# The down projection of a decoder trunk by seven half-size products, with weights moving and tokens as rows

## The chip, the cores and the metric

One core of one Trainium2 chip runs the whole trunk. The metric is device time in microseconds from launch to end; lower is better. Three runs of the kernel before were timed, and one further execution was profiled.

## The reference

For 512 tokens of width 2048 the trunk computes a token mixer, a residual, a SwiGLU feed-forward block, a second residual and a last RMSNorm, all in float32. The change concerns the second half:

```python
    h = h + mix @ w_out                       # (512, 2048), w_out (2048, 2048)
    xn = rms_norm(h, ffn_norm_w)
    ff = silu(xn @ w_gate) * (xn @ w_up)      # (512, 5632)
    h = h + ff @ w_down                       # w_down (5632, 2048)
    return rms_norm(h, final_norm_w)
```

## The kernel before

**Precision.** A float32 operand is split into a rounded part and a rest, both in the format fp32r (`split`: ScalarE writes the first, VectorE subtracts for the second), and each product takes three TensorE instructions (`mm3`, lines 147 to 149): high by high, high by low, low by high. In the names of the trace `wh`, `wl` are the parts of a weight tile, `hh`, `hl` those of the normed input, `sh`, `sl` those of its sums, `fh`, `fl` those of the feed-forward activations. "mm<-fh,wh" names the moving operand first and the standing one second.

**Layout.** Activations lie with features on the 128 partitions and 512 tokens along the row. Weight tiles stand in the array and tokens move, in most stages. In the early stage of `rows_tiles` it is the other way: tokens stand, weights move.

**Stages.** `project` computes h + mix @ w_out in 16 tiles of 128 features; it stores h to DRAM (`hd`, from ScalarE's queue), keeps a copy times the norm's weights (`hf`) and the split parts (`hw`), and sums squares on GpSimd. `project_end` adds the squares over partitions on TensorE and makes the norm's factors. The norm's division is applied later: gate and up are multiplied by `rstd`, h is multiplied by `rms`, and the last norm divides both out.

Gate/up then runs over 44 tiles f, each with one gate and one up tile of 128 columns. The first two are plain (`ff_plain`). The other 42 (`ff_fast`) halve tokens, contraction and the pair gate/up, and replace eight half-size products by seven, with sums of the operands: the token sums are made once (`token_sums`), the weight sums per tile on VectorE (lines 784, 786, 787, 794). Four raw weight tiles of 128x1024 give seven split weight tiles. The order of the products is 11, 12, S2, S1, S3, 22, S4; two of the four PSUM banks accumulate more than one product, so that a bank must be read between two of them. `put_ff` (lines 732 to 735) applies the norm and silu, and stores u to DRAM (`ffd`, 256 KB, from SP's queue).

Down (`down_all`) loads h back (16 loads of 256 KB on ScalarE's queue), multiplies it by `rms` (line 895), loads the activations in chunks of eight tiles and splits them (`ff_load`), and for each chunk runs the 16 output tiles, eight k-tiles each, with an add into h (line 816). The last chunk of four tiles (`down_last`) runs over two token halves of 256, so that the last norm of the first half lies beside the products of the second. The last norm is squares on ScalarE, a sum on VectorE, one TensorE instruction over partitions, a small chain, and a multiplication per tile; the stores go out on SP's and ScalarE's queues.

**Order and buffers.** Instructions are traced in program order; a scheduler then fixes each engine's order by priority and by its own estimate of time. `high_priority(offset=6000)` lets weight loads, sums and splits run ahead of what the program has before them; a negative offset holds work back. Each engine works its queue in that fixed order. Ahead of the products run three split weight tiles (`wh`, `wl`, three buffers each) and five raw ones. A new tile in a buffer's place waits until the readers of the old one are done.

Of the kernel before, what the change touches and what calls it, by code (L numbers as in the profile page):

```python
# [27 lines left out]
GF = 4  # L28
CF = 8
NCHUNK = NF // CF  # L30
PLAIN = 2
HALF = 256
NB = S // P
# [11 lines left out]
POOL_OUT = (0, 4)  # L45
# [8 lines left out]
def _layout_cols():  # L54
    at = 0
    for name, n in (
        ("attn_w", 16), ("q_w", 4), ("kv_w", 4), ("mla_w", 1), ("conv_w", 4 * CONV_W),
        ("conv_b", 4), ("ln_w", 4), ("ln_b", 4), ("lower", HG), ("hgrn_w", 1),
        ("ffn_w", 16), ("final_w", 16), ("inv_freq", 1), ("sign", 1), ("eps", 1),
        ("ln_eps", 1), ("half_pi", 1),  # L60
    ):
        _COLS[name] = (at, n)
        at += n
    return at
# [30 lines left out]
class Trunk:  # L95
# [574 lines left out]
    def project(self, w, r4):  # L670
# [3 lines left out]
        self.hd = self.dp.tile([KT, P, S], F32, name="hd")  # L674
        sq_sum = self.sq_sum = r4("acc")
        for m in range(KT):
            t = self.hf[:, m]
            nc.sync.dma_start(t, self.io["x"][m])
            bank = self.cols_tile(w, self.mix_y + self.mix)
            nc.vector.tensor_tensor(t, t, bank, op=ALU.add)  # L680
            nc.scalar.dma_start(self.hd[m], t)
            self.hw.append(self.split(t, self.hp("hh", F32R), self.hp("hl", F32R), self.col("ffn_w", m)))
            if m == 0:
                nc.scalar.activation(sq_sum, t, AF.Square)
            else:
                q = r4("sq")
                nc.scalar.activation(q, t, AF.Square)
                nc.gpsimd.tensor_tensor(sq_sum, sq_sum, q, op=ALU.add)
            nc.scalar.activation(t, t, AF.Copy, scale=self.col("ffn_w", m))

    def project_end(self, r4):
# [3 lines left out]
        y, q, v = r4("sq"), self.rstd, r4("acc")  # L695
        nc.vector.tensor_scalar(self.rms, total, 1.0 / D, self.col("eps"), op0=ALU.mult, op1=ALU.add)
        r = self.rsqrt(total, D, "eps", v, y, q)
        nc.vector.tensor_scalar(self.epsv, self.rms, EPS, None, op0=ALU.mult)
        nc.vector.tensor_tensor(self.rms, self.rms, r, op=ALU.mult)
        nc.vector.tensor_copy(self.rstd, r)  # L700
# [3 lines left out]
    def token_sums(self, sp, tp):  # L704
# [4 lines left out]
        H = {i: (sp("sh", F32R, (P, n, HALF)), sp("sl", F32R, (P, n, HALF))) for i in (1, 2, 3, 4)}  # L709
# [19 lines left out]

    def put_ff(self, f, g, u):  # L730
# [4 lines left out]
        nc.sync.dma_start(self.ffd[f], u)  # L735

    def ff_plain(self, f, w, fp):
        nc = self.nc
        gbank = self.cols_tile(w, self.hw)
        ubank = self.cols_tile(w, self.hw)  # L740
        g, u = fp("g"), fp("u")
# [3 lines left out]
        nc.sync.dma_start(self.ffd[f], u)  # L745

    def ff_fast(self, f, w, rp, fp):
# [4 lines left out]
        with self.tc.high_priority(offset=6000):  # L752
            b11, b21, b12, b22 = raws = [rp("raw", F32, W) for _ in range(4)]
# [21 lines left out]
        g, u = fp("g"), fp("u")  # L775
# [7 lines left out]
        def sums():  # L783
            tt(b11, b12, b11, op=ALU.subtract)
            t2 = rp("t2", F32, W)
# [16 lines left out]
        self.put_ff(f, g, u)  # L802


    def ff_load(self, k, fp):
        nc = self.nc
        with self.tc.high_priority(offset=3000):
            t = fp("fr")
            nc.scalar.dma_start(t, self.ffd[k])
            return self.split(t, fp("fh", F32R), fp("fl", F32R))  # L810

    def down(self, w, ff):
        nc = self.nc
        for m in range(KT):
            bank = self.cols_tile(w, ff)
            nc.vector.tensor_tensor(self.h[:, m], self.h[:, m], bank, op=ALU.add)  # L816

    def down_last(self, w, ff, r5, lp):

        nc = self.nc  # L820
        self.tables_after(self.last_silu)
        wt = []
        for m2 in range(KT // 2):
            if m2 < 3:
                h, l = self.weights(next(w))
                wt += [(h[:, :S], l[:, :S]), (h[:, S:], l[:, S:])]
            else:
                raw = self.wp.tile([P, 1024], F32, tag="raw", name="raw", bufs=2)
                nc.sync.dma_start(raw, next(w))
                for s in (slice(0, S), slice(S, 2 * S)):  # L830
                    wt.append(self.split(raw[:, s], lp("wlh", F32R), lp("wll", F32R)))
        n = S // 2
        acc = r5("acc")
        for th in range(2):
            ts = slice(th * n, (th + 1) * n)
            for m in range(KT):
                bank = self.ps("mm")[:, :n]
                for k in range(GF):
                    s = slice(k * P, (k + 1) * P)
                    self.mm3(bank, (wt[m][0][:, s], wt[m][1][:, s]), (ff[k][0][:, ts], ff[k][1][:, ts]),  # L840
                             k == 0, k == GF - 1)
                hm = self.h[:, m, ts]
                nc.vector.tensor_tensor(hm, hm, bank, op=ALU.add)
                if m == 0:
                    nc.scalar.activation(acc[:, ts], hm, AF.Square)
                else:
                    q = r5("sq", F32, (P, n))
                    nc.scalar.activation(q, hm, AF.Square)
                    nc.vector.tensor_tensor(acc[:, ts], acc[:, ts], q, op=ALU.add)
            scaled = {}  # L850
            for m in POOL_OUT:
                scaled[m] = o = lp("mx")
                for i in range(2):
                    nc.scalar.activation(o[:, i * n:(i + 1) * n], self.h[:, m + i, ts], AF.Copy,
                                         scale=self.col("final_w", m + i))
            bank = self.ps("ax")[:, :n]
            nc.tensor.matmul(bank, self.ones, acc[:, ts], start=True, stop=True)
            r = self.rsqrt_of(bank, self.epsv[:, ts], r5("v", F32, (P, n)), r5("y", F32, (P, n)), r5("sq", F32, (P, n)))
            for m in range(0, KT, 2):
                if m in scaled:  # L860
                    o = scaled[m]
                    ob = o.rearrange("p (m s) -> p m s", m=2)
                    nc.gpsimd.tensor_tensor(ob[:, 0], ob[:, 0], r, op=ALU.mult)
                    nc.gpsimd.tensor_tensor(ob[:, 1], ob[:, 1], r, op=ALU.mult)
                    self.put_out(m, ts, o)
                    continue
                o = lp("mx")
                for i in range(2):
                    nc.vector.scalar_tensor_tensor(  # L869
                        o[:, i * n:(i + 1) * n], self.h[:, m + i, ts], self.col("final_w", m + i), r,  # L870
                        ALU.mult, ALU.mult)
                self.put_out(m, ts, o)
# [11 lines left out]

    def put_out(self, m, ts, o):
        (self.nc.sync if m % 4 else self.nc.scalar).dma_start(
            self.io["out"][m:m + 2, :, ts].rearrange("m p s -> p m s"), o.rearrange("p (m s) -> p m s", m=2))

    def down_all(self, w, fp, r5, lp):

        nc = self.nc
        ff = [self.ff_load(k, fp) for k in range(CF)]
        for m in range(KT):
            nc.scalar.dma_start(self.h[:, m], self.hd[m])
# [8 lines left out]
    def run(self):  # L903
# [76 lines left out]
        for f in range(PLAIN):  # L980
            self.ff_plain(f, wg, fp)
# [132 lines left out]
```

## Time and profile before

| | us |
|---|---|
| median of three runs | 2116.49 |
| lowest, highest | 2115.91, 2147.79 |
| the profiled execution | 2116.3 |
| its span, first to last instruction | 2114.5 |
| mean granted TensorE clock of the span | 0.988 of full |

The profile comes from one execution, so that sums made from its rows are held against its own 2116.3 us. That lies within 0.2 us of the median.

### The profile page before, as it was taken

Reading aid. Unit: us, or ns where it says so; the run is one execution under the profiler, and the core shown is the slowest. Engines: PE = TensorE matmul, PEld = TensorE weight load, DVE = VectorE, ACT = ScalarE, POOL = GpSimd, SP = SyncE. Lnnn points to the kernel's source line nnn. Section 1 sums busy time; section 2 is a strip of 40 time slices with the busy share of each in tenths; the row PEclk is TensorE's granted clock in tenths of the full one; section 3 lists DMA queues with packets and bytes.
Section 4 is the critical chain, followed back from the end, with each engine's and each line's share of the span. In section 5 each row is a group of like instructions: output and inputs, shape, how many; then the busy total and the mean of one; then the engine's idle time right before and its main releaser. Section 6 shows DMA issues by size and latency. Waiting matters only on the chain.

```text
span 2114.5 us, 31918 instructions
## 1 busy us (share of the span) xinstructions
PE 2059.7 (97%) x13060; PEld 1853.3 (88%) x13060; DVE 1390.6 (66%) x1787; ACT 891.5 (42%) x1353; POOL 174.4 (8%) x152
## 2 busy tenths in 40 slices
PE   8999999999999999999999999999997999999996
PEld 6888888878878879999999999999995888888886
DVE  7897685466643377877887778877886344343347
ACT  6323764357553344444444444444443222221223
POOL 4102475100011100000000000000000000000001
PEclk9999999999999999999999999999998999999998
DMA  5233422322253333344334443344336343342332
GB/s 187 90 120 109 141 80 80 98 84 70 66 186 123 125 129 110 116 135 135 119 113 129 135 129 114 118 135 135 118 102 223 106 139 119 115 135 100 104 101 99
DMA packets 89907, 252.43 MB, mean 119 GB/s; under 512 B 9424, under 2 KB 17872, under 8 KB 89760
## 3 DMA queue, kind: packets, MB, share of 16 engines
q1 hardware_dynamic: 76528, 228.00, 33.8%
q10 hardware_dynamic: 13120, 22.03, 3.0%
q8 instruction: 102, 1.67, 0.3%
q0 software_dynamic: 112, 0.36, 0.1%
q14 instruction: 45, 0.37, 0.1%
HBM read 226.24 MB, written 24.12 MB: 118 GB/s over the span
## 4 chain that ended last, share of the span: by engine, by line
PE 90%; DVE 3%; ACT 3%; DMA 2%; POOL 1%; issue 1%; SPq 0%; DVEq 0%; ACTq 0%; POOLq 0%
PE mm L147 28%; PE mm L149 28%; PE mm L148 28%; PE lv L377 1%; PE ob L618 1%; PE lv L149 1%; PE lv L148 1%; PE lv L147 1%; DVE mx L869 1%; ACT wh L138 0%; DMA fr<-ffd 0%; DVE wl L139 0%; PE tb L610 0%; DMA xraw<-in_x 0%; POOL ps L367 0%
## 5 line engine op out<-in xcount | busy, mean ns | idle before, releaser
L138 ACT CAST wh<-raw 128x1024 fp32r<-128x1024 f32 (+1 forms) x463 | 478.6, 1035 | 808.8 <-PE mm L148 737.3
L139 DVE TENSOR_TENSOR wl<-raw,wh 128x1024 fp32r<-128x1024 f32 (+1 forms) x463 | 569.2, 1231 | 291.2 <-ACT wh L138 290.9
L147 PE MATMUL mm<-sh,wh 128*128 128x256 f32 x1344 | 369.0, 276 | 0.1
L148 PE MATMUL mm<-sl,wh 128*128 128x256 f32 x1344 | 368.9, 276 | 0.0
L149 PE MATMUL mm<-sh,wl 128*128 128x256 f32 x1344 | 364.2, 276 | 0.0
L147 PE MATMUL mm<-hh,wh 128*128 128x256 f32 (+1 forms) x1072 | 304.6, 284 | 0.0
L149 PE MATMUL mm<-hh,wl 128*128 128x256 f32 (+1 forms) x1072 | 304.3, 284 | 0.0
L148 PE MATMUL mm<-hl,wh 128*128 128x256 f32 (+1 forms) x1072 | 304.1, 284 | 0.0
L147 PE MATMUL mm<-fh,wh 128*128 128x512 f32 (+1 forms) x688 | 262.8, 386 | 13.4 <-ACT fh L138 9.7
L149 PE MATMUL mm<-fh,wl 128*128 128x512 f32 (+1 forms) x688 | 264.5, 385 | 0.5 <-DVE wl L139 0.5
L148 PE MATMUL mm<-fl,wh 128*128 128x512 f32 (+1 forms) x688 | 264.4, 384 | 0.5 <-DVE fl L139 0.5
L147 PEld LDWEIGHTS mm<-sh,wh 128*128 128x128 f32 x1344 | 252.3, 188 | 0.3 <-DVE u L797 0.3
L148 PEld LDWEIGHTS mm<-sl,wh 128*128 128x128 f32 x1344 | 252.3, 188 | 0.0
L149 PEld LDWEIGHTS mm<-sh,wl 128*128 128x128 f32 x1344 | 249.1, 188 | 0.0
L816 DVE TENSOR_TENSOR h<-h,mm 128x512 f32<-128x512 f32 x80 | 55.0, 689 | 239.4 <-PE mm L149 239.4
L147 PEld LDWEIGHTS mm<-hh,wh 128*128 128x128 f32 x1072 | 201.7, 188 | 3.3 <-issue 0.2
L148 PEld LDWEIGHTS mm<-hl,wh 128*128 128x128 f32 x1072 | 201.7, 188 | 3.3 <-issue 0.2
L149 PEld LDWEIGHTS mm<-hh,wl 128*128 128x128 f32 x1072 | 201.5, 188 | 3.0
L147 PE MATMUL mm<-xh,wh 128*128 128x512 f32 x400 | 161.1, 403 | 6.5 <-ACT wh L138 6.4
L147 PEld LDWEIGHTS mm<-fh,wh 128*128 128x128 f32 x688 | 130.5, 190 | 39.9 <-ACT fh L138 10.4
L148 PE MATMUL mm<-xl,wh 128*128 128x512 f32 x400 | 159.6, 399 | 2.1 <-DVE xl L142 2.1
L149 PE MATMUL mm<-xh,wl 128*128 128x512 f32 x400 | 157.5, 397 | 0.0
(330 smaller groups left out, 3235.5 us busy)
## 6 DMA issues: line engine op xcount, KB each, us to landing
raw<-in_w_gu SPq DMA_DIRECT2D x176, 512.0 KB, 4.3
raw<-in_w_down SPq DMA_DIRECT2D x88, 512.0 KB, 3.3
raw<-in_w_cols SPq DMA_DIRECT2D x42, 512.0 KB, 3.4
raw<-in_w_out SPq DMA_DIRECT2D x32, 512.0 KB, 3.3
ffd<-u SPq DMA_DIRECT2D x44, 256.0 KB, 3.9
fr<-ffd ACTq DMA_DIRECT2D x44, 256.0 KB, 3.7
raw<-in_w_rows SPq DMA_DIRECT2D x16, 512.0 KB, 3.3
raw<-in_w_attn SPq DMA_DIRECT2D x14, 512.0 KB, 3.4
```

Of the source, the lines that this page charges most:

```text
L138: nc.scalar.copy(h, src)
L139: nc.vector.tensor_tensor(l, src, h.bitcast(F32), op=ALU.subtract)
L147: mm(out, a[0], b[0], start=first, stop=False, **k)
L148: mm(out, a[0], b[1], start=False, stop=False, **k)
L149: mm(out, a[1], b[0], start=False, stop=last, **k)
L377: nc.tensor.matmul(bank[:, c * 64:(c + 1) * 64], e[:, c * P:(c + 1) * P], ap_of(e, c * P + h, [2 * h, 64 // h], [1, h]), start=True, stop= ...
L618: nc.tensor.matmul(obank[:, qs], pt[:, js], vt[h // 4, j][:, hs], start=j == 0, stop=j == i)
L816: nc.vector.tensor_tensor(self.h[:, m], self.h[:, m], bank, op=ALU.add)
L869: nc.vector.scalar_tensor_tensor(o[:, i * n:(i + 1) * n], self.h[:, m + i, ts], self.col("final_w", m + i), r, ALU.mult, ALU.mult)
```

## The change

**Down.** Tokens, contraction and output columns are halved, and seven half-size products take the place of eight, with the same sums as in gate/up. Token forms stand in the array in blocks of 128 tokens, weights move 512 columns at a time, and the output has tokens on the partitions. The 22 pairs of k-tiles are cut into chunks of 6, 6, 6 and 4 (`CHUNKS`). Each chunk has two blocks of 1024 output columns (`mb`), and a block has half as many units as its chunk has pairs: a unit is four raw weight tiles, which give seven split ones by four sums on VectorE (`weight_sums`). Each product runs over all units of its block before the next begins. Twelve buffers hold the raw tiles of a block; the third sum `t2` has two. The products add into `acc`, four tiles of 128 tokens by 2048, with 16 adds of 512 columns per block; the first add to each place also multiplies by `rms`.

**Forms.** Gate/up now writes two tiles' u side by side in one tile `form`. After each pair `put_forms` makes the three further sums' forms (four sums of 256 columns), splits all seven (1024 and 768 columns) and stores both parts to DRAM, 0.9 MB each in pieces of 1 KB, from SP's queue. `form` and `fh` have one buffer. Its priority is held back by 150. Down loads the forms already split, 14 loads per chunk, on SP's queue between the weight loads, in the order of the products.

**Around it.** `project` adds a transposition of h per tile (`turn`: four TensorE transposes, a ScalarE copy, a store in pieces of 512 bytes on SP's queue); the first gate product is traced ahead of `project_end`; `acc` is loaded by four loads of 1 MB on GpSimd's queue. Raw buffers in gate/up are four and two in place of five and one; `g`, `pc` have one buffer. The tiles of gate/up's area are named and laid out in the order in which the last tile frees them. The last norm is per token: squares with a sum along the row on ScalarE, factors of one column, and the multiplication by the norm's weights on VectorE, token block by token block.

```diff
+CHUNKS = ((0, 6), (6, 6), (12, 6), (18, 4))
+FORMS_LATER = 150
...
+    def turn(self, m, t, r4, tag="tb"):
+        nc = self.nc
+        bank = self.ps(tag)
+        for c in range(NB):
+            s = slice(c * P, (c + 1) * P)
+            nc.tensor.transpose(bank[:, s], t[:, s], self.ident)
+        o = r4("t")
+        nc.scalar.copy(o, bank)
+        nc.sync.dma_start(self.hd[:, :, m * P:(m + 1) * P].rearrange("c p f -> p c f"),
+                            o.rearrange("p (c f) -> p c f", c=NB))
...
+    def ff_tile(self, f, fp):
+        if f % 2 == 0:
+            self.form = fp("form", F32, (P, 7 * HALF))
+        return self.form[:, (f % 2) * S:(f % 2 + 1) * S]
...
-        nc.sync.dma_start(self.ffd[f], u)
+    def put_forms(self, j, fp):
+        x = self.form
+        at = lambda i: x[:, i * HALF:(i + 1) * HALF]
+        with self.tc.high_priority(offset=-FORMS_LATER):
+            tt(at(4), at(1), at(3), op=ALU.add)
+            tt(at(1), at(0), at(1), op=ALU.subtract)
+            tt(at(5), at(4), at(0), op=ALU.subtract)
+            tt(at(6), at(2), at(5), op=ALU.subtract)
+            h = fp("fh", F32R, (P, 7 * HALF))
+            l = x[:].bitcast(F32R)
+            for s in (slice(0, 4 * HALF), slice(4 * HALF, 7 * HALF)):
+                nc.scalar.copy(h[:, s], x[:, s])
+                tt(l[:, s], x[:, s], h[:, s].bitcast(F32), op=ALU.subtract)
+            for part, t in enumerate((h, l)):
+                nc.sync.dma_start(self.ffd[part, :, :, j * HALF:(j + 1) * HALF].rearrange("f p c -> p f c"),
+                                  t.bitcast(F32).rearrange("p (f c) -> p f c", f=7))
...
+            extra = lambda: self.wp.tile([P, 1024], F32, tag="raw", name="raw", bufs=2)
+            b11, b21, b12, b22 = raws = [extra()] + [rp("raw", F32, W) for _ in range(3)]
...
+    def down_block(self, w, A, at, n, rp, tp, add, last=False):
+        def product(banks, ts, name, start=True, by_sub=False):
+            mine = A[name]
+            def step(b, hl, i, p):
+                s = slice(p * S, (p + 1) * S)
+                k = 2 * i + p
+                x = slice(k * HALF + b * P, k * HALF + (b + 1) * P)
+                self.mm3(banks[b], (mine[0][:, x], mine[1][:, x]), (hl[0][:, s], hl[1][:, s]),
+                         start and k == 0, k == n - 1, skip_group_check=not start)
...
+        def loads():
+            b11 = load()
+            forms("11")
+            b21 = load()
+            forms("12")
+            b12 = load()
+            b22 = load()
+            forms("S2", "S1", "S3", "22", "S4")
+            return b11, b21, b12, b22
...
+        product(one, b11, "11")
+        put((0, 0), one)
+        product(two, b21, "12")
+        put((0, 0), two)
+        product(one, Sums(), "S2", start=False)
+        put((0, 1), one)
+        product(three, b11, "S1")
+        put((1, 1), three)
+        product(one, b12, "S3", start=False)
+        put((1, 0), one)
+        put((1, 1), one)
+        product(four, b21, "22")
+        put((1, 0), four, ALU.subtract)
+        product(three, b22, "S4", start=False, by_sub=last)
+        put((0, 1), three)
...
+        wg = stream("w_gu")
+        gbank = self.cols_tile(wg, self.hw)
+        self.turn(KT - 1, h15, r4, "mm")
         self.project_end(r4)
...
-        self.ps = area("banks4", {"mm": 6, "ax": 2}, space=PSUM)
+        tp = area("forms", {n + x: 1 for n in ("11", "12", "S2", "S1", "S3", "22", "S4") for x in "hl"})
+        rp = area("raw12", {"raw": 12}, "right")
+        ap = area("acc", {"acc": NB}, "right")
```

## Rows read from the trace of the kernel before

**Rows 1.** Page, part 1: busy us, share, instructions.
```profile
PE 2059.7 (97%) x13060; PEld 1853.3 (88%) x13060; DVE 1390.6 (66%) x1787; ACT 891.5 (42%) x1353; POOL 174.4 (8%) x152
```

**Rows 2.** Windows: us; busy (starts) by engine; granted clock, DMA share, GB/s.
```profile
180.00:200.00 20.00, 20.00 (x88) 16.20 (x87) 12.09 (x15) 10.27 (x16) 2.90 (x2) 1.00 0.33 105
1200.00:1400.00 200.00, 200.00 (x1767) 200.00 (x1766) 160.49 (x179) 91.01 (x117) 0.00 (x0) 1.00 0.41 127
1600.00:1620.00 20.00, 13.06 (x46) 10.03 (x47) 13.71 (x22) 5.52 (x8) 0.00 (x0) 0.74 0.84 310
1800.00:2040.00 240.00, 240.00 (x1060) 198.77 (x1059) 92.28 (x101) 53.53 (x57) 0.00 (x0) 1.00 0.34 109
```

**Rows 3.** TensorE's timeline around down: start, us, line, [idle before <- releaser].
```profile
1596.40 0.28 PE L149 MATMUL mm<-sh,wl 128*128 128x256 f32 x1
1606.41 1.22 PE L147 MATMUL mm<-fh,wh 128*128 128x512 f32 x2 [9.73 <-ACT fh L138]
...
1629.52 0.50 PE L147 MATMUL mm<-fh,wh 128*128 128x512 f32 x1 [3.43 <-ACT wh L138]
...
2097.51 0.28 PE L149 MATMUL mm<-fh,wll 128*128 128x256 f32 x1
```

**Rows 4.** VectorE's timeline through one gate/up tile.
```profile
1213.87 0.41 DVE L799 TENSOR_TENSOR g<-pc,mm 128x256 f32<-128x256 f32 x1
...
1216.47 1.22 DVE L794 TENSOR_TENSOR raw<-raw 128x1024 f32<-128x1024 f32 x1
1217.60 0.69 DVE L732 TENSOR_TENSOR g<-g,rstd 128x512 f32<-128x512 f32 x1
1218.20 1.22 DVE L787 TENSOR_TENSOR raw<-t,raw 128x1024 f32<-128x1024 f32 x1
...
1221.94 0.69 DVE L734 TENSOR_TENSOR u<-u,g 128x512 f32<-128x512 f32 x1
...
1224.86 1.23 DVE L139 TENSOR_TENSOR wl<-raw,wh 128x1024 fp32r<-128x1024 f32 x1 [0.76 <-ACT wh L138]
1227.35 1.23 DVE L139 TENSOR_TENSOR wl<-raw,wh 128x1024 fp32r<-128x1024 f32 x1 [1.27 <-ACT wh L138]
1230.30 1.23 DVE L139 TENSOR_TENSOR wl<-raw,wh 128x1024 fp32r<-128x1024 f32 x1 [1.72 <-ACT wh L138]
1231.44 0.42 DVE L797 TENSOR_TENSOR u<-pc,mm 128x256 f32<-128x256 f32 x1
1231.77 1.22 DVE L784 TENSOR_TENSOR raw<-raw 128x1024 f32<-128x1024 f32 x1
```

**Rows 5.** Groups by line: count, busy us, mean ns, idle before.
```profile
L138 ACT CAST wh<-raw 128x1024 fp32r<-128x1024 f32 x227 | 238.5, 1051 | 238.7 <-PE mm L148 237.1 <-DMA raw<-in_w_down 1.7
...
L816 DVE TENSOR_TENSOR h<-h,mm 128x512 f32<-128x512 f32 x77 | 53.1, 689 | 239.4 <-PE mm L149 239.4
```

**Rows 6.** DMA: GB/s from 1590 to 1640; issues, median us to landing.
```profile
GB/s 0 0 0 108 293 392 341 383 346 356 410 403 405 421 393 390 383 392 387 275 11 23 187 182 236 205 105 187 179 185 0 187 211 21 249 233 264 342 331 252
...
ffd<-u SPq DMA_DIRECT2D x44, 256.0 KB, 3.9
...
hd<-hf ACTq DMA_DIRECT2D x16, 256.0 KB, 2.0
...
lmask<-in_lmask POOLq DMA_DIRECT2D x1, 288.0 KB, 5.7
```

**Rows 7.** TensorE's timeline in attention: two transposes in a row.
```profile
492.88 0.27 PE L642 MATMUL tb<-ident,og 128*128 128x128 f32 x1
492.99 0.27 PE L610 MATMUL tb<-ident,p 128*128 128x128 f32 x1
```

**Rows 8.** TensorE's timeline between project and gate/up.
```profile
749.10 1.13 PE L199 MATMUL mm<-acc,ones 128*128 128x512 f32 x2 [3.95 <-POOL acc L688]
...
751.01 0.63 PE L147 MATMUL mm<-hh,wh 128*128 128x512 f32 x1
751.44 0.63 PE L148 MATMUL mm<-hl,wh 128*128 128x512 f32 x1
```

More of the change, by code (lines that the diff above doesn't have):

```diff
@@ L694, in project_end @@
         total = self.sum_over_partitions(self.sq_sum, "mm")
[L695 to L697 removed]
+        bank = self.ps("mm")
+        for c in range(NB):
+            nc.tensor.matmul(bank[:, c:c + 1], self.sq_sum[:, c * P:(c + 1) * P], self.ones[:, :1],
+                             start=True, stop=True)
+        y, q, v = r4("t"), r4("h"), r4("acc")
+        nc.vector.tensor_copy(self.rstd, self.rsqrt(total, D, "eps", v, y, q))
+        r = self.rsqrt_small(bank[:, :NB], D)
+        nc.vector.tensor_scalar(self.rms, bank[:, :NB], 1.0 / D, self.col("eps"), op0=ALU.mult, op1=ALU.add)
         nc.vector.tensor_scalar(self.epsv, self.rms, EPS, None, op0=ALU.mult)
         nc.vector.tensor_tensor(self.rms, self.rms, r, op=ALU.mult)
[L700 removed]
     def token_sums(self, sp, tp):
@@ L802, in ff_fast @@
         self.put_ff(f, g, u)
-    def ff_load(self, k, fp):
+        if f % 2:
+            self.put_forms(f // 2, fp)
+    def down_block(self, w, A, at, n, rp, tp, add, last=False):
         nc = self.nc
[L807 to L812, printed above, removed]
-        nc = self.nc
-        for m in range(KT):
-            bank = self.cols_tile(w, ff)
-            nc.vector.tensor_tensor(self.h[:, m], self.h[:, m], bank, op=ALU.add)
@@ L818, in down_last @@
-    def down_last(self, w, ff, r5, lp):
-        nc = self.nc
-        self.tables_after(self.last_silu)
[L822 to L872, printed above, removed]
@@ new lines, in down_block, with early, load, forms @@
+        W = (P, 1024)
+        units = range(n // 2)
+        def early(f, *a):
+            with self.tc.high_priority(offset=6000):
+                return f(*a)
+        def load():
+            out = []
+            for _ in units:
+                t = rp("raw", F32, W)
+                nc.sync.dma_start(t, next(w))
+                out.append(t)
+            return out
+        def forms(*names):
+            for name in names:
+                if name not in A:
+                    A[name] = []
+                    for part in range(2):
+                        t = tp(f"{name}{'hl'[part]}", F32R, (P, n * HALF))
+                        nc.sync.dma_start(t.bitcast(F32), self.ffd[part, FORMS[name], :, at * HALF:(at + n) * HALF])
+                        A[name].append(t)
@@ new lines, in loads, with put @@
+        def loads():
[7 more added lines that the diff above has]
+            return b11, b21, b12, b22
+        b11, b21, b12, b22 = early(loads)
+        two_banks = lambda: [self.ps("mm") for _ in range(2)]
+        one, two, three, four = (two_banks() for _ in range(4))
+        def put(q, banks, op=ALU.add):
+            for b in range(2):
+                add(q, b, banks[b], op)
```

165 lines of the change are left out of this document (106 added, 59 removed).

## The prediction

> **What bounds the kernel now.** I read the page's busy shares first: TensorE 97%, VectorE 66%, ScalarE 42% of 2114.5 us [rows 1]. A busy TensorE need not be a dense one, so the windows by stage came next [rows 2]. In gate/up 1767 products of 256 columns start in 200 us, 0.1132 us each, at a granted clock of 1.00; in down 1060 products of 512 columns start in 240 us, 0.2264 us each. The spacing doubles with the columns and every product has its weight load beside it (1766, 1059), so TensorE is dense there and time is count times spacing. VectorE works 160.5 of the 200 us in gate/up and 92.3 of the 240 us in down: room to note, since the change spends it. What is left are holes at the joints, read from TensorE's timeline.
>
> Down before: five chunks of 16 x 8 x 3 products are 1920 x 0.2264 = 434.7 us; the last chunk, cut into token halves, is 384 x 0.1132 = 43.5; together 478.2. From the last gate/up product (1596.5) to the last of down (2097.6) pass 501.1 us [rows 3], so the joint and small waits lose 22.9: TensorE waits 9.73 us for the first split activations and 3.43 us for a weight split, and the granted clock in between averages 0.74 [rows 2, 3], so part of it ran at 1.2 GHz. From 2097.6 to the end of the span are 16.9 us of tail.
>
> **The products.** A half-size product of down has 22 k-tiles, 2 token blocks, 2 column blocks and 3 terms: 264 instructions of 512 columns; seven make 1848 where there were 1920 + 384 halves (2112 whole ones). Whether weights may move and tokens stand is answered by an earlier stage that already does so: 88 products in 20 us, 0.2273 [rows 2]. I take 0.2264, 418.4 us: **-59.8** (-58.1 at 0.2273).
>
> **VectorE in down.** Two instructions of 1024 columns start 1.135 us apart, one of 512 takes 0.60 (starts 1216.47, 1217.60, 1218.20) [rows 4], and an add out of PSUM lasts as long as another of its size (689 ns) [rows 5]. Four loads make a unit: seven splits and four sums, 11 x 1.135 = 12.5 us of VectorE against 84 x 0.2264 = 19.0 of TensorE. A block of three units adds 16 accumulations, 9.6 us: 47.1 against 57.1. The last two blocks have two units: 34.6 against 38.0. So on average TensorE still binds, at 82 and 91% VectorE. The demand is uneven, though: the third product takes 8.2 us of TensorE, and its three units want 17.0 us of VectorE (four sums and a split each). Work may run ahead, because twelve raw tiles hold a whole block, but the sum has two buffers and a split only three, and in the first block of each chunk the weights for the sums come behind form loads. From below: all hidden, 0. From above: half of the difference lost in every block, 4.4 us in six and 2.9 in the two short ones, 32. I take **+6**, near the lower end, because gate/up has the same 11 to 84 ratio and shows no hole. ScalarE has 7 x 1.05 us per unit [rows 5], no bound.
>
> **Forms made in gate/up.** Each pair of gate/up tiles adds four sums of 256 (0.33 each by 1231.44 to 1231.77), splits of 1024 and 768 columns (1.135 + 0.87 on VectorE): 3.3 us per pair, 1.7 per tile. VectorE is now idle 0.76 + 1.27 + 1.72 us per tile [rows 4], so they fit, at 88%. The wait is in the buffers. There is one form tile; the next pair's upper half of u may be written only when the DMA that reads it has landed. Tile boundaries: the fourth product is read at 1213.87, the last product ends 2.7 us later, 1216.5; u is final at 1221.94 + 0.69 = 1222.6; the next tile's write of u is at 1231.44 and its last product, which accumulates on the same bank, starts at 1232.9, 16.4 us after the pair's end. Four sums, copy and split in VectorE's gaps end at about +13.5 (estimate: 6.1 + 1.3 + 1.05 + 2.0 + 3 of others' turns). Then 1.835 MB go out in 1 KB pieces: at the 400 GB/s that the busiest slices show [rows 6], 4.6 us, or 7.8 beside weight loads that hold 0.41 of the queues [rows 2], + 2.0 to land (shortest store, `hd` [rows 6]): +23, some 7 us late. TensorE can fill that with the next tile's products (2.7 us each; its banks are free and splits have three buffers) if the queue order puts them ahead; VectorE, in order, must then have that write behind the next splits too. All filled: 0; nothing filled: 21 x 7 = 147. I take **+5**: the write needs nothing that the next tile's first products want. The SP queue holds these stores between weight loads: 44 of 0.9 MB in place of 44 of 256 KB.
>
> **The joint into down.** The 16 loads of h, 16 multiplications and 44 activation splits go, with the 9.73 us wait that they end. In their place SP loads b11, form 11, b21, form 12 and so on, into space that the last tile frees product by product: b11 from 16 us and form 11 from 11 us before its end. Before the third product seven sets of 1.57 MB and half of acc (2.1 MB, on GpSimd's queue) must be in, 16 us after the joint; 13.1 MB at 390 GB/s (the full slices in the middle of today's joint [rows 6]) take 33.6 us of 16 + 16. So about balanced; VectorE's sums then follow late by a few us. Lost: 22.9 before, I take 6 (2 if all lands ahead; 27 if form 11 waits for the last pair's store, +20 and a load of 6): **-17**. GpSimd's queue showed one large load, 5.7 us for 288 KB [rows 6], late enough to be harmless: acc is first read 8 us in.
> The Trainium skill (DMA: Bandwidth & Descriptors, Specifications) gives about 358 GB/s as HBM's limit for a core; by it the same 13.1 MB would take 36.6 us and the joint lose 3 us more. The slices of this trace at 383 to 421 GB/s differ, and they decide.
>
> **Project.** 64 transposes at 0.11 us (two starts [rows 7]) are +7.0; ScalarE's extra copy and SP's 16 stores in 512-byte pieces lie beside 10.9 us of products per tile. At the joint behind it TensorE now waits 3.95 us for GpSimd, then runs some ten products 0.43 apart, the 1.2 GHz level (2 us lost) [rows 8]; the first gate product moves ahead of it: -6. **+1** (-2 to +7).
>
> **Tail.** Now 16.9. Then: last add 0.6, square, a chain of five small instructions, scaling of 4 x 2 x 1.2 us and 4.2 MB of stores, 10.7 us at 390 GB/s + 2. Half of it starts a product earlier. I take 13 (10 to 17): **-4**.
>
> **Sum**, against the profiled execution, 2116.3 (span + 1.8; the median of the runs is 2116.5, so no correction): 2116.3 - 59.8 + 6 + 5 - 17 + 1 - 4 = **2047.5**, 3.3% less. Best ends: 2116.3 - 59.8 + 0 + 0 - 21 - 2 - 7 = 2026.
>
> **Rivals.**
> *The form store stops the next pair* (slower than before). Mechanism: the write of u waits in VectorE's queue for the store, splits stand behind it, TensorE runs dry. It decides from the point where the store lands later than 16.4 us after the pair plus what TensorE can fill. Nothing filled: 2042 + 147 = 2190; half filled 2116. For: one buffer, 88% VectorE, 1 KB pieces. Against: deep room to fill, and 256 KB stores now disturb nothing.
> The Trainium skill (DMA: Bandwidth & Descriptors, Anatomy of one DMA) gives about 2.0 us fixed, mostly the receipt from the target memory, plus bytes over 436 GB/s. An estimate by it: 6.2 us for the pair's store, landing at +20, 3 to 4 us late: 75 us without fill. The median 3.9 us for 256 KB here [rows 6] is longer than its 2.6.
> *VectorE binds in down*: clustered sums cost their upper bound, 2047.5 + 26 = 2073. For: 82 to 91%; against: the ratio in gate/up.
> *The joint stays*: form loads wait for the last store; 2047.5 + 21 = 2069. For: one tensor takes all stores and loads; against: the first chunk's loads touch other parts of it than the last store writes.
> *The products aren't denser*: standing tokens reload as often as before, so nothing beyond count is gained; at a spacing of 0.26 the stage would take 480 us and the whole 2110. The 0.2273 of [rows 2] speaks against.
>
> **Numbers.** Chances: forecast (2026 to 2065) 0.60; VectorE binding 0.13; joint 0.10; store wait 0.14, half of it slower than before; spacing 0.03. The range 2029 to 2105 leaves out the worse part of the store wait and the best end, under 2 in 10. About 2% (42 us) is what a measurement of this kernel can tell from no change. Faster by over 2% (below 2074): forecast, most of joint and VectorE: 0.76. Within: 0.19. Slower by over 2%: 0.05.
>
> **What would show it.** 1848 products of down at 0.226 and the down stage 425 to 432 us long; gate/up tiles still 19.04 us apart (more: the store wait, with u's write idle before a DMA); the joint without a wait of 9 us; VectorE idle for weight splits, not TensorE for VectorE, at each third product; transposes within 7 us. The prediction is wrong if TensorE has holes before the S2 products or before each second tile's last product.

## The result, and the profile after

The changed kernel takes **2138.49 us** (2135.6 to 2140.18), against 2116.49 before: ratio 1.0102, 95% interval 1.0086 to 1.0119. I had forecast 2047.5 and a range that ends at 2105. The profiled execution took 2135.6 us (span 2133.7), 19.2 more in span than the one before. In some executions of kernels whose weight tiles lie as in the kernel before, that kernel among them, the time is some 31 us longer, and where such an execution was profiled (e11, e12, e14, e14b and the shift by 256 bytes) the 256-column products stand 117.8 ns apart throughout; these executions are left out of the ratios and of the times below, and of their profiles only the joint and down are read.

Of the kernel after, the page's busy shares, then windows by stage (columns as in [rows 2]; the third one is the joint):
```profile
PE 2042.7 (96%) x12672; PEld 1829.9 (86%) x12672; DVE 1607.2 (75%) x1991; ACT 974.1 (46%) x1415; POOL 167.3 (8%) x148
```
```profile
1200.00:1400.00 200.00, 195.81 (x1660) 194.79 (x1660) 170.14 (x200) 94.26 (x119) 0.00 (x0) 1.00 0.46 149
1651.00:1711.00 60.00, 28.25 (x99) 22.28 (x100) 32.29 (x34) 11.79 (x13) 2.13 (x4) 0.69 0.90 362
1800.00:2040.00 240.00, 236.63 (x1031) 192.04 (x1031) 197.31 (x200) 88.97 (x87) 0.00 (x0) 1.00 0.55 193
```
The first line looks harmless: TensorE is as busy as before. The windows are not. In gate/up, where the change gives TensorE nothing to do, 1660 products start where 1767 did [rows 2], at the same granted clock of 1.00, though TensorE stands for only 4.2 of the 200 us. So the products that do run stand further apart: 113.3 ns before, **117.8** now. In the joint TensorE works 28 of 60 us while the DMA engines are 0.90 busy.

The timeline of the kernel after, all engines, rows picked in order of time:
```profile
797.83 0.28 PE L147 MATMUL mm<-hh,wh 128*128 128x256 f32 x1
...
1221.53 0.36 ACT L844 COPY pc<-mm 128x256 f32<-128x256 f32 x1
...
1227.11 1.05 ACT L138 CAST wh<-raw 128x1024 fp32r<-128x1024 f32 x1 [0.67 <-DVE raw L834]
...
1228.81 0.28 PE L148 MATMUL mm<-sl,wh 128*128 128x256 f32 x1
1228.83 1.05 ACT L138 CAST wh<-raw 128x1024 fp32r<-128x1024 f32 x1 [0.67 <-PE mm L148]
...
1229.53 0.41 DVE L845 TENSOR_TENSOR form<-pc,mm 128x256 f32<-128x256 f32 x1
...
1229.93 0.39 PE L147 MATMUL mm<-sh,wh 128*128 128x256 f32 x1 [0.84 <-ACT wh L138]
...
1233.30 0.42 DVE L849 TENSOR_TENSOR form<-pb,mm 128x256 f32<-128x256 f32 x1 [1.08 <-PE mm L149]
...
1649.06 0.70 SPq L880 DMA_DIRECT2D 11h<-ffd  x1
...
1650.72 0.28 PE L149 MATMUL mm<-sh,wl 128*128 128x256 f32 x1
...
1658.29 0.76 PE L147 MATMUL mm<-wh,11h 128*128 128x512 f32 x1 [7.29 <-DMA 11h<-ffd]
...
1675.64 0.32 SPq L880 DMA_DIRECT2D S4l<-ffd  x1
1677.57 0.37 SPq L779 DMA_DIRECT2D ffd<-fh  x1
1679.46 0.37 SPq L779 DMA_DIRECT2D ffd<-form  x1
...
1695.97 2.13 POOL L964 DMA_DIRECT2D acc<-hd  x4 [939.42 <-DMA ffd<-form]
...
1701.08 0.75 DVE L979 SCALAR_TENSOR_TENSOR acc<-acc,rms,mm 128x512 f32<-128x512 f32 x1 [14.93 <-DMA acc<-hd]
...
1701.93 0.76 PE L147 MATMUL mm<-wh,S2h 128*128 128x512 f32 x1 [24.46 <-issue]
...
2117.65 0.39 PE L149 MATMUL mm<-wh,S4l 128*128 128x512 f32 x1
```
Two things are to be seen. In gate/up (the rows at 1221 to 1233) two starts of TensorE lie 1.12 us apart, 1228.81 and 1229.93, and the second waits for a split on ScalarE. That split waited in its turn for TensorE (`mm L148`): there are three buffers for these halves of a split, and product 12, which read its own until 1228.7, had held the one that is taken. The sum for S2 is not what is waited for: its split runs from 1227.11 to 1228.16, and the product that reads it starts on time at 1228.70. What stands otherwise than before is S4 of the pair's first tile. It adds into the bank that VectorE's L845 reads; L845 writes into `form`, had its operand `pc` at 1221.9 and runs at 1229.53. So S4 comes behind 12 of the next tile (from 1230.27; L849 reads its result at 1233.30), where in the kernel before, and here in each pair's second tile, it stands between 11 and 12. Such a stop comes once in a pair, 19 times; with one of 2.6 us at the start of this part and one of 0.5 us they are 21, which lose 21.9 us. At the joint the row that says "issue" has its cause in the rows above it. S2 adds into the bank of the first product; that bank is first read by VectorE's add into `acc`; the add waits for the acc load; GpSimd could issue this only when the last store of `form` had landed, since acc lies where `form` lay; and SP issued that store behind ten loads of forms.

From first to last product the 256-column part of gate/up takes 852.9 us (797.83 to 1650.72; before 800.0), down 466.9 to its last product (before 501.1), the tail 16.0 (before 17.0), and what lies ahead of gate/up 1.4 more: +52.9 - 34.2 - 1.0 + 1.4 = +19.1, the 19.2 of the span but for rounding.

### The profile page after: what moved, and what is told of

It reads as the page before. It is cut to its first block, busy times and chain, and to the rows that moved or that the text cites. A ratio compares the mean times of both kernels' runs of the same rounds, so it can differ in the third digit from the quotient of the medians.

```text
span 2133.7 us, 31591 instructions
## 1 busy us (share of the span) xinstructions
PE 2042.7 (96%) x12672; PEld 1829.9 (86%) x12672; DVE 1607.2 (75%) x1991; ACT 974.1 (46%) x1415; POOL 167.3 (8%) x148
## 4 chain that ended last, share of the span: by engine, by line
PE 86%; DVE 6%; ACT 2%; issue 2%; DMA 2%; POOL 1%; DVEq 0%; SPq 0%; ACTq 0%; POOLq 0%
PE mm L147 26%; PE mm L148 26%; PE mm L149 26%; DVE wl L139 2%; ACT wh L138 1%; PE lv L377 1%; PE ob L618 1%; PE lv L147 1%; PE lv L149 1%; PE lv L148 1%; DMA xraw<-in_x 1%; DVE raw L954 1%; DVE raw L955 1%; DVE raw L956 1%; DMA raw<-in_w_down 1%
## 5 line engine op out<-in xcount | busy, mean ns | idle before, releaser
L138 ACT CAST wh<-raw 128x1024 fp32r<-128x1024 f32 (+1 forms) x576 | 593.6, 1037 | 905.1 <-PE mm L148 438.7
L139 DVE TENSOR_TENSOR wl<-raw,wh 128x1024 fp32r<-128x1024 f32 (+1 forms) x576 | 700.2, 1226 | 306.1 <-ACT wh L138 302.9
L147 PE MATMUL mm<-sh,wh 128*128 128x256 f32 x1344 | 377.3, 282 | 16.2 <-ACT wh L138 15.9
L148 PE MATMUL mm<-sl,wh 128*128 128x256 f32 x1344 | 374.9, 280 | 0.0
L148 PE MATMUL mm<-hl,wh 128*128 128x256 f32 (+1 forms) x1072 | 306.4, 286 | 0.0
L148 PEld LDWEIGHTS mm<-sl,wh 128*128 128x128 f32 x1344 | 253.4, 189 | 0.0
L148 PEld LDWEIGHTS mm<-hl,wh 128*128 128x128 f32 x1072 | 201.6, 188 | 2.7
L148 PE MATMUL mm<-xl,wh 128*128 128x512 f32 x400 | 158.8, 397 | 0.0
L147 PE MATMUL mm<-mx,wh 128*128 128x512 f32 x256 | 101.3, 399 | 0.8 <-ACT mx L141 0.8
L148 PE MATMUL mm<-mx,wh 128*128 128x512 f32 x256 | 100.6, 393 | 0.0
L149 PE MATMUL mm<-mx,wl 128*128 128x512 f32 x256 | 100.6, 393 | 0.0
L147 PEld LDWEIGHTS mm<-xh,wh 128*128 128x128 f32 x400 | 76.6, 191 | 22.5 <-ACT wh L138 5.8
L148 PEld LDWEIGHTS mm<-xl,wh 128*128 128x128 f32 x400 | 76.8, 192 | 16.0 <-issue 0.7
```

The costliest lines, as they stand in the source:

```text
L138: nc.scalar.copy(h, src)
L139: nc.vector.tensor_tensor(l, src, h.bitcast(F32), op=ALU.subtract)
L147: mm(out, a[0], b[0], start=first, stop=False, **k)
L148: mm(out, a[0], b[1], start=False, stop=False, **k)
L149: mm(out, a[1], b[0], start=False, stop=last, **k)
```

## The experiments

**e1_tags: the place of the weight tiles.** The tail's three small tiles take tags that exist, which moves the weight tiles back by 384 bytes. The token tiles `hh`, `hl` are placed from the other end of memory and stay.
```diff
-*[self.small(f"e{i}", 1) for i in range(3)]
+*[self.small(f"r{i}")[:, :1] for i in range(3)]
```


> The tail's three small tiles for the reciprocal root (12 buffers of 32 bytes) are taken from tags that exist already, which moves every weight buffer and all that lies left of the middle back by 384 bytes; nothing else changes. Theory A (place): the products of 256 columns stand 117.8 ns apart instead of the 113.3 of the kernel before because the weight tiles now lie otherwise against the token tiles hh and hl, whose place did not shift with them. Then they return to 113.3 ns: 42 tiles x 168 x 4.5 ns = 32 us, about 2107 us, and the 1.1 us stop of each pair of tiles stays (a pair at 39.1 us instead of 40.6). Rival B (stops): TensorE falls into the slower spacing after it has stood, so the stop of each pair keeps it there. Then nothing changes: 117.8 ns and 2138 us.

Measured: 2125.9 us, ratio 1.0044 (1.0030 to 1.0058). 4895 of the 7055 starts are back at 113.3 ns and 2063 stand at 117.8. The spacing changes at stops alone: six of the twenty stretches from one stop to the next, some 330 products each, are at 117.8 from end to end, the others at 113.3. The part takes 838.3 us, 14.6 less, where all at 113.3 had promised 32. Neither theory alone: the place decides whether 113.3 can hold, and a stop can end it until the next stop.

**e6_before384: the place alone, in the kernel before.**
```diff
-        cp.tile([P, 8], F32, name="pad")
+        cp.tile([P, 8 + 96], F32, name="pad")
```


> The kernel before with nothing changed but an unused tile made 384 bytes longer, which moves the weight buffers and everything left of the middle as far as the change moved them. Theory A (place alone sets the spacing): the 7056 products of 256 columns go from 113.3 to 117.8 ns, no stop appears, and the time is 32 us longer, about 2148 us. Rival: the spacing comes from something else that the change brought (forms, other buffers of the token tiles): nothing moves, 2116 us.

Measured: 2143.19 us, 1.0121 (1.0105 to 1.0137). Its window:
```profile
1200.00:1400.00 200.00, 200.00 (x1709) 200.00 (x1708) 154.10 (x171) 87.01 (x112) 0.00 (x0) 1.00 0.40 123
```
TensorE is busy 200.00 of 200 us, there is no stop and no form, and 58 products fewer start than in [rows 2]. The part takes 826.7 us, 26.7 more. Place alone does it.

**e16_before64, e16_before128, e16_before256: how far.** The same unused tile, longer by 16, 32 and 64 elements.

> The kernel before with an unused tile 64 bytes longer, so that the weight buffers and all left of the middle lie 64 bytes further. If what matters is the exact distance between weight tiles and token tiles, any shift breaks it: 117.8 ns, about 2143 us as with 384 bytes. If only the distance modulo a larger unit matters, 64 bytes may change nothing: 113.3 ns, 2118 us.

> The same with 128 bytes. 384 is an odd multiple of 128: if the unit is 256 bytes, this run is slow like the one with 384, 117.8 ns and 2143 us; if it is 128 bytes or fewer it cannot tell, since 384 would then be a whole number of units and should not have been slow.

> The same with 256 bytes. If the unit is 256 bytes, nothing changes: 113.3 ns, 2118 us. If it is 512 or more, or the exact distance counts: 117.8 ns, 2143 us.

Measured: 64 bytes 2148.45 us, 128 bytes 2145.73, 256 bytes 2117.7. The window of the first; that of the second has 1709 starts, as e6:
```profile
1200.00:1400.00 200.00, 200.00 (x1704) 200.00 (x1703) 155.39 (x175) 87.47 (x112) 0.00 (x0) 1.00 0.39 119
```
64, 128 and 384 bytes cost 25 to 30 us, 256 nothing: of the units that these four shifts can tell apart, 256 bytes fits.

**e3_nowork: the forms' arithmetic left out.** `put_forms` keeps only its two stores, of the tile as it stands.
```diff
-            tt(at(4), at(1), at(3), op=ALU.add)
...
-                tt(l[:, s], x[:, s], h[:, s].bitcast(F32), op=ALU.subtract)
+            h = l = x
```


> The forms are not computed in gate/up: the four sums, two casts and two subtractions of each pair are left out, and the tile as it stands is stored for both parts; the two stores and every later step stay, so the output is of other forms. Theory A (place of the weight tiles sets the spacing, VectorE's extra work sets the stop): the 1.1 us stop of each pair goes, 21 us less, but the spacing stays at 117.8 ns: 2117 us. Rival B (stops set the spacing): both go, 52 us less, 2086 us. Rival C (the stores, not the arithmetic, cause the loss): nothing changes, 2138 us.

Measured: 2120.07 us. The part takes 835.7 us, 17 less; 9 stops of 7.2 us in sum are left where there were 21 of 21.9, and most of the spacing stays at 117.8. So theory A: of the stops that wait for ScalarE's half of a split one is left of 19, at the start of the part; the other eight wait for VectorE's half. With most of the standing time gone the spacing does not come back.

**e4_twou: a second buffer for the pieces.** The four pieces that gate/up writes get two buffers, the three sums a tile `more` of their own (4 KB more in all, which were free).
```diff
-FORMS_LATER = 150
+FORMS_LATER = 400
...
-            self.form = fp("form", F32, (P, 7 * HALF))
+            self.form = fp("form", F32, (P, 4 * HALF))
...
+            y = fp("more", F32, (P, 3 * HALF))
...
-fp = area("gu", {"g": 1, "form": 1, "fh": 1,
+fp = area("gu", {"g": 1, "form": 2, "more": 1, "fh": 1,
```


> The arithmetic of the forms is kept, but the four pieces that the next pair writes have two buffers (the three sums a tile of their own), and the priority of this work is lowered from 150 to 400 instructions behind. Theory A: the stop of 1.1 us is one of order alone, since VectorE does the forms ahead of the weight sums that S2 waits for; it has the time for both. With room to put them later the stop goes: 21 us less, 2117 us at an unchanged spacing of 117.8 ns. Rival (VectorE is short of time whatever the order): the stop moves to another product and a pair still takes 40.6 us: 2138 us. Rival B of the spacing: with the stop gone it is 113.3 ns and the time 2086 us.

Measured: **2103.15 us**, 0.9933 (0.9917 to 0.9949). With all the arithmetic kept, of TensorE's stops only the one of 2.6 us at the start of the part is left:
```profile
1200.00:1400.00 200.00, 200.00 (x1705) 200.00 (x1705) 172.72 (x203) 94.85 (x120) 0.00 (x0) 1.00 0.48 152
```
The spacing stays at 117.8, as theory A had it; the part takes 832.9 us, 20 less. S4 stands between 11 and 12 in every tile again. The buffers did it, not the priority: with 150 in place of 400 the program that is built is the same. The second buffer and the tile of its own came together, and no run parts them. Another 15 us came unasked in down (452.1): SP now issues the last stores ahead of the form loads, and acc's stop is gone, though the first one is 20 us in its place.

**e5_tags_twou: both.** 

> The two edits that worked on gate/up together: the weight buffers back by 384 bytes and the double-buffered pieces with the forms at 400 behind. The stops were found to put the spacing at 117.8 ns for a while even in the right place, and the wrong place to give 117.8 ns without any stop. Theory A (both are needed): every product of 256 columns at 113.3 ns, a pair of tiles at 38.1 us as in the kernel before, 32 us below 2103: 2071 us. Rival: with products 4% faster VectorE is short of time, stops come back and the spacing with them: 2090 to 2105 us.

Measured: **2075.33 us**, 0.9800 (0.9783 to 0.9818).
```profile
1200.00:1400.00 200.00, 200.00 (x1767) 200.00 (x1767) 178.91 (x211) 99.01 (x126) 0.00 (x0) 1.00 0.52 166
```
1767 products, as before, with the forms made beside them at 89% VectorE. The part takes 804.0 us. Alone the edits gave 14.6 and 20.0 us there, together 48.9 of the 52.9 lost; of the 4 left, 2.5 are the stop at its start. Gate/up is explained but for these; the rest of the gap to the forecast is the joint.

**e2_pool: the last stores alone.** On the kernel after, the last pair's stores go through GpSimd's queue.
```diff
-                nc.sync.dma_start(self.ffd[part, :, :, j * HALF
+                (nc.gpsimd if j == NP - 1 else nc.sync).dma_start(self.ffd[part, :, :, j * HALF
```


> Only the last pair's two stores of forms go out on GpSimd's queue instead of SP's, where they stood behind ten loads of forms. Theory A: the four acc loads waited for these two stores alone, so they start near 1668 us instead of 1696, the hole of 24.5 us at 1677 goes and so does the half clock after it: about 28 us less, 2110 us; the 7.3 us wait for the first form at 1658 stays. Rival: the acc loads then share the transfers with the form loads, the forms land later and the hole comes back in front of a later product: 0 to 10 us less, 2128 to 2138 us.

Measured: 2122.09 us, 16 less, between the two. acc's loads start at 1674 and not at 1696, the stop in front of S2 falls from 24.5 to 11.9 us: the store was the cause, but issued at 1660 it still lands 13 us later, among the other transfers.

**e8, e10 to e13c: other queues, other places.** All stand on e5. e8: forms 11, 12, S1 of the first chunk through GpSimd's queue, acc in halves, S1 multiplied ahead of S2. e10: forms 11, 12 through GpSimd's and the last stores through ScalarE's queue. e11: e10 with S1 ahead of S2. e12: e10 with the chunks as 4, 6, 6, 6. e13_acc_apart: acc's first two tiles over `hl`, not over `form`, forms 11, 12 and S1 through GpSimd's queue, S1 ahead of S2 in the first block alone. e13c: the same, S2 third and its forms on GpSimd's queue in place of S1's.

> As the run with both gate/up edits, and the first block of down is fed in the order of its needs: the forms 11, 12 and S1 of the first chunk go through GpSimd's queue instead of SP's (where twelve weight loads and the last stores stand ahead of them), acc is loaded in halves, and S1 is multiplied before S2, so that the third product needs one more block of weights and not two, and VectorE makes one sum in front of it and not all four. Theory A (the joint is a matter of the order in which 21 MB come in, at the 410 to 420 GB/s that the joint shows): the stop before the first product falls from 20 us to under 8, no second one, and the short stops in front of S2 in the steady part shrink: 15 to 25 us below the run with both gate/up edits. Rival (the transfers themselves bind: 11 MB of forms, 6 MB of weights and 4 MB of tokens in the first 57 us): the stop moves behind a later product and no more than 5 us are won.

> As the run with both gate/up edits (2075 us), with the joint's queues parted: forms 11 and 12 of the first chunk through GpSimd's queue, the last pair's stores through ScalarE's, acc in halves on GpSimd's behind those forms; the products keep their order. Theory A (what stands ahead in the queue sets the stop): the forms start some 15 us before the end of gate/up, acc some 15 us earlier, and of the 21.6 us of stops at the joint about 6 are left: 2058 to 2062 us. Rival (the 410 to 420 GB/s that the joint already shows bind, whatever the order): the stop comes back in front of S2, which needs two more blocks of weights and its own forms, and the sum of the stops stays above 14 us: 2068 us or more.

> As the run with the queues parted, and S1 is multiplied before S2. Theory A: with the queues parted, acc comes in time and the third product wants 3.1 MB and not 4.7, so the stop in front of it is 6 to 8 us shorter than there; the steady part of down pays some 3 us for the later sums, as the run with S1 first showed: 3 to 5 us less than with the queues parted alone. Rival (the stop had been acc's alone): no shorter stop, 3 us more.

> As the run with the queues parted, with the four blocks of 4 rows taken first and not last. The first block then needs 7 MB of forms and 4 MB of weights in 38 us of products, and not 11 and 6 MB in 57 us. Theory A (bytes bind at the joint): per microsecond it needs hardly fewer bytes and the half of acc comes on top, so the stops stay within 3 us of that run; the end is 2 to 3 us later, since the last block has three weight tiles to finish and not two. Rival (latency binds: the wait for the first transfers, not their sum): smaller transfers land sooner and 5 us or more are won.

> As the run with both gate/up edits, and at the joint acc is taken off the last store: its first two tiles lie over the token tiles hl and not over the forms' tile, so they can be loaded before the last store has landed; forms 11, 12 and S1 of the first chunk and acc go through GpSimd's queue, and S1 stands before S2 in the first block alone. Theory A (acc's place binds: VectorE stands in its queue at the first sum into acc until the last store and the acc load behind it are done, and the weights' splits stand behind that): the stops at the joint fall from 21 to under 8 us and nothing is paid later: 2058 to 2064 us. Rival (the transfers bind at 410 GB/s whatever waits for them): the stops stay above 14 us, 2068 us or more.

> The same with the products in their old order (S2 third) and the forms 11, 12 and S2 through GpSimd's queue. If acc's place alone binds, it gives the same as the run with S1 first, 2058 to 2064 us. If the two more blocks of weights that S2 needs bind, it has a stop of 5 us or more in front of S2 that the other has not: 2064 to 2070 us.

Measured: 2075, 2078.7, 2085.2, 2082.2, 2075.8 and 2074 us; e5 has 2075.3. None won more than 1.5 us, and e10, e11 and e12 lost 3 to 10. Summed over the first 75 us of down, what the starts of products lose against 0.2267 us is 17.4 (e8), 25.9 (e10), 26.6 (e12), 23.4 (e13) and 22.7 us (e13c), against 21.9 in e5; what e8 won there it lost again in later blocks. The stops moved, from form 11 to a split of 12, to acc, to S2. The rivals ("the transfers bind") named the times, and I took the cause to be bytes. But 17 us for one form of 768 KB while 410 GB/s flow is a queue, not a size; so the last runs put all loads in the order of need.

**e14_need_order, e14b: one queue in the order of need.** On e13_acc_apart and e13c: each load of the first block's weights and forms, and of half of acc, is tied behind the one that is needed before it, all on SP. The last stores and the other half of acc go through GpSimd's queue. No run parts the order from the move of the stores.
```diff
+        def queued(ins):
+            if first and self.queue is not None:
+                self.after(ins, self.queue)
+            if first:
+                self.queue = ins
...
+            forms("11")
             b11 = load()
-            forms("11")
             b21 = load()
             forms("12")
+            if first:
+                for c in (0, 1):
+                    queued(nc.sync.dma_start(self.acc[c][:, :2 * S], self.hd[c, :, :2 * S]))
```


> As the run with acc apart and S1 first in the first block, and the first block's loads stand on SP's queue in one order, that of the products' needs, and stay in it: forms 11, six weight blocks, forms 12, the first quarter of acc, three weight blocks, forms S1, three weight blocks, forms S2 and so on; the last stores and the rest of acc go through GpSimd's queue. Theory A (what is in flight shares the 410 GB/s, so that what was queued early and is needed late holds up what is needed first): the first form lands 4 to 6 us after its issue and not 17, the first stop falls from 17 us to under 4 and the sum of stops to 5 to 8 us: 2060 to 2064 us. Rival (the bytes bind in any order): the stops only move to S1 or S2 and stay at 14 us or more in sum: 2068 us or more.

> The same order of need with the products as they were, S2 third with its two more weight blocks and its forms. Theory A: 12 MB must have landed before S2, at 410 GB/s 29 us after the first issue at about 1596, while TensorE is there some 24 us after it: a stop of 4 to 6 us more than with S1 first, 2064 to 2069 us. Rival (bytes in any order): the same 2068 us or more as there.

Measured: **2067.3 us**, 0.9761 (0.9740 to 0.9782), the fastest of all; e14b 2069.7, 0.9776. The DMA views of e13_acc_apart and of e14 from 1590 to 1670, form 11's load: KB, median us from issue to landing.
```profile
11h<-ffd POOLq DMA_DIRECT2D x1, 768.0 KB, 17.4
```
```profile
11h<-ffd SPq DMA_DIRECT2D x1, 768.0 KB, 4.3
```
The first stop falls from 17.1 to 5.0 us, the sum from 23.4 to 14.9. Theory A had 5 to 8 and 2060 to 2064, so it is right in kind and half in size; the sum that is left is the rival's, 14 or more, and the time lies 0.7 us below the rival's. The first stop that is left, from e14's timeline:
```profile
1640.35 2.93 ACT L138 CAST wh<-raw 128x1024 fp32r<-128x1024 f32 x3
...
1641.44 1.22 PE L147 MATMUL mm<-wh,11h 128*128 128x512 f32 x2 [4.98 <-ACT wh L138]
```
These 5.0 us are not a load's: the first weight tile was issued at 1626.28 and landed 6.5 us later, but its split stands in ScalarE's queue behind those of the last pair's forms and starts at 1640.35. Then come 4 to 5 us in small stops at S1 and S2, and starts at half clock behind them (granted clock 0.50 from 1641 to 1645, 0.69 from 1672 to 1676). From 1636 to 1696 the DMA engines are busy all the time; that these bytes set the rest is likely, but no run took bytes away.

## Why the prediction was wrong, step by step

**Forms in gate/up, +5: wrong, 52.9.** Two causes. The failed step of the first is "TensorE can fill that with the next tile's products", with "splits have three buffers" as its reason and 5 us as its price. The store did land late, 19.1 us after the pair's end (issued at 1220.88, landed 7.1 us later; the pair ends at 1208.8), where 16.4 was the limit. And TensorE did fill: S4, which has to wait for the write of u, was put behind 12 of the next tile. But then 12 still held the third split buffer when the split behind S2's wanted one, and TensorE stood for that split's 1.1 us, 19 times: with the two other stops 21.9 us. e4, with a second buffer, has S4 back in its place and none of the 19. The rival had u's write wait in VectorE's queue for the store's landing; that wait is 0.9 us in all, in two pairs, because VectorE's order had put other work ahead of it. The rival's times (2116 to 2190) hold the measured one by luck.

The other 31 us I could not have had from the count of operations: 5949 starts stood 117.8 for 113.3 ns apart, some 26 us, because small tiles for the tail, at the far end of the kernel, had moved the weight tiles by 384 bytes, a distance that is no multiple of 256 (e6, e16); the rest is in still slower starts, most of them behind the stops. My own tests in the text, gate/up tiles 19.04 us apart or more and holes before each second tile's last product, caught the loss; the explanation given with the first, u's write idle before a DMA, would have been wrong.

**Joint, -17: wrong, +17.** By the starts of products it lost 20.8 before and 37.6 after. The failed step is the sentence that GpSimd's queue is "late enough to be harmless". I asked when acc is read and not what its place waits for: acc lies over `form` and `fh`, whose last reader is the last store, and this stood on SP behind ten loads that were themselves waiting. The rival that form loads wait for the last store had the right store and the wrong waiter. The sum of 13.1 MB over 16 + 16 us had two more faults. That the bytes come in the order of need was assumed; e14 shows what that is worth, the move of the last stores with it: 8 us. And the first 16 us were not there: one weight tile was issued at 1631.14, the next at 1646.32 and form 11 at 1649.06, where I had 16 and 11 us before the last product at 1650.72; from 1631.0 to 1646.3 the DMA engines moved 36 GB/s. By an estimate from these rows, 12.6 MB at the 410 GB/s of the joint take 31 us from 1646.3 on and end 26 us after gate/up, against 16 us of products: some 10 us are lost even in the order of need, where I took 6 for the whole. For the rate I took 390 GB/s; e13's slices in the joint mostly show 403 to 430. The Trainium skill (HBM Reference, Specifications) says that a core streaming alone measures about 425 GB/s; that agrees with these slices, and the 358 that I set beside my sum does not.

**Products, -59.8: right.** 1848 products, in undisturbed stretches 0.2267 us apart: 418.9 us against 478.2, -59.3. Weights may move and tokens stand at the same spacing as the other way round.

**VectorE in down, +6: right in kind.** The starts behind the first 75 us lose 10.3 us, most of it in stops of 1.2 us in front of S2, once per block, and near them. VectorE works 197 of 240 us (82%, as worked out). The upper bound of 32 did not come near.

**Project, +1: within its bounds.** 1.4 in this profile; in those of e1 to e14, the same program up to there but for e1's shift, the first product of 256 columns starts 3 to 8 us later than in the kernel before. That kernel, with its tiles shifted (e6, e16), starts it 1.3 us earlier to 3.9 later, so that this term cannot be told more closely. The 3.95 us wait [rows 8] is gone, the transposes cost it back.

**Tail, -4: too much**, 1.0 gained. The last product ends at 2118.0, and the span ends 15.6 us later: two waves of squares on ScalarE and eight scalings of 1.2 us on VectorE follow in a row, as the last of them starts at 2128.1, and the last store then still has to land.

Together: +1.4 + 52.9 - 34.2 - 1.0 where I had +1 + 5 - 70.8 - 4. With gate/up mended (e5) 28 us are left to the forecast: 16 in the joint (21.9 for 6), 4 in down's small stops, 3 in the tail, 5 ahead of gate/up. With the joint in order (e14) they are 20, of which the joint has 9.

## What to carry to other kernels

When an edit adds or drops small tiles, compare where the operands of the hot products lie before and after (modulo 256 bytes, as far as these shifts show), even if the tiles belong to another stage; if products slow down with no wait and a full clock, move them by an unused tile. Price a single buffer by the order that it forces on the engines, and by the other buffers that this order holds longer, not by the wait at its gate alone; for a load ask what its destination's last reader waits for, and what stands ahead of that in its queue. Where a stage begins with many loads, put them on one queue in the order of need: what was queued early and is needed late shares the transfers with what is needed now.

## What the runs showed of the hardware that I had not expected

Products of 256 columns have two spacings at one granted clock of 1.00, 113.3 and 117.8 ns. At the place of the kernel before, one of them holds from stop to stop: 7030 starts in a row at 113.3 in its profile, 7031 at 117.8 in that of the shift by 256 bytes, and in e1 some 330 at a time, with a change at stops alone. With the weight tiles (and all that lies left of the middle) shifted by 64, 128 or 384 bytes against `hh` and `hl` the long one came in each of the 22 executions timed; beside the shifts by 64 and 128 bytes, 21 of 32 executions at 0 and 256 bytes had, by their times, the short one. But even at the bad places it did not come for every product: one of the seven of a tile stands at 113.4 there, S4 in e6, in the shift by 128 bytes and in half of the tiles of the kernel after. Down's products, where weights move, stood 0.2267 apart in both places. What in the chip makes the two spacings, whether the long one has the same cause at the good place and at the bad ones, and whether the distance to `hh`, to the sums or the weights' own address counts, no run here tells apart.

A load's landing time was set by what was in flight before it: 768 KB took 4.3 us at the head of the queue (e14) and 17.4 behind weights and acc (e13).
